# A two-layer trunk on one core: head and tail in another order, three gate tiles, memory values in other PSUM tiles, and the inverse copied in other pieces

## The chip, the core and the metric

The kernel runs on one core of one Trainium2 chip. A core has five engines that run side by side: TensorE (PE, matmul, with PEld for its weight loads), VectorE (DVE), ScalarE (ACT), GpSimd (POOL) and SyncE (SP, which issues the transfers here). The metric is the device time of one execution in microseconds; the kernel before takes 1491.95 us (median of three runs, 1491.53 to 1492.02).

## The reference

The input x is 512 tokens by 1024, the memory is 256 tokens by 1024, all in f32. Two layers follow each other. Cut to what is computed:

```python
for l in range(2):
    h = x @ w_in[l]                      # columns shared out to four branches, their gates and the merge gates
    y_rwkv = _rwkv7_branch(...)          # delta-rule state, 8 heads of 64
    y_mla  = _mla_branch(...)            # latent attention, 8 heads, rotary key
    y_conv = _conformer_conv_branch(...) # GLU, causal convolution of width 31, layer norm, silu
    y_mem  = _memory_xattn_branch(xq, xg, mem, xattn_w_mem_kv[l])   # k, v = mem @ w_mem_kv
    branches = jnp.stack([y_rwkv, y_mla, y_conv, y_mem], axis=2)
    proj   = jnp.einsum('bsnc,ncd->bsnd', branches, w_o_branch[l])
    gates  = jax.nn.sigmoid(merge.reshape(B, S, N_BRANCH, D) + b_gate[l])
    merged = jnp.sum(gates * proj, axis=2)
    x = _layer_norm(DEEPNORM_ALPHA * x + merged @ w_out[l], ln_g[l], ln_b[l])
```

## The kernel before

**Order of the work.** The class Plan (line 67) is a planner. The kernel is written as many small generators (tasks); the planner keeps one clock for each of PE, ACT, DVE and POOL, adds a cost for each operation, and always takes the task that is due next. The order that comes out is the program order on each engine. A plan.spawn(task) hands in a task, plan.t is the time from which it is due, and a yield gives the turn back. So an edit of a cost, a due time or a yield can move instructions far from it. How an engine really waits is decided by semaphores that the framework puts in between.

**Products.** Every f32 matrix is split into a high half (rounded to f32r) and a low half (the rest), and a product is three matmuls, high by low, high by high and low by high. Weights arrive by SP into a raw tile (tag wr, two of them); weights (line 437) then splits them: ACT casts w..h, DVE subtracts w..l. The tiles of x become xh and xl in the same way. The first weight, w0, arrives in two halves in one raw tile, w00 and w01; these and w1 to w7 are the latent projection pl, whose eight steps k use w and x of the same number k (w0's halves stand for k = 0 and 1, and w1 for k = 2 and 3, and so on).

**PSUM.** Three pools share the eight banks: pp (2 banks), pa (2) and pg (4, or 2 while the RWKV branch runs with its small matmuls). A PSUM tile is free for the next user when the engine that reads it is done.

**The memory branch.** Key products (ps_mk) and value products (pmv) of layer 2 are computed at the end of layer 1, by keys and values (line 604). Each product is split from PSUM by ACT (kmh, vmh) and DVE (kml, vml).

**Gates.** In each layer 32 merge gates go through `gate`: a projection ps_m, then a tanh on ACT into a tile tm of tag tg. When the branch's output projection po is done, DVE forms (tm + 1) po, for the first branch into merged, for the others into a tile mt of tag mt, which it adds to merged right after. Tag tg has two tiles and is used by the GLU of the convolution (tglu) and the branch gates too; tag mt has two and is used by the rotary key (kr) as well.

**RWKV in chunks.** In each of eight units the inverse of a small triangular matrix is built by products: x0 gives P and its transpose PT, x1 gives PP and QQ, x2 gives Zi and a half of RA. The other parts (BP, the other half of RA) come from y0. These are read from PSUM by ACT and DVE in turn. State products S come from w on DVE, and tk is PE's transpose of v into the bank that S frees.

**The end of a layer.** `norm` (line 1812) runs per block tb of 128 tokens: pz, the output projection, is added to z by DVE in four quarters, statistics are taken (lbs, lmv), POOL computes lrs, the reciprocal standard deviation, DVE then lnb, and ACT, DVE and POOL apply lrs, ln_g and ln_b. In layer 1 the result is stored and transposed (xT) to be the x of layer 2; in layer 2 each quarter z31, say (block 3, quarter 1), is stored.

## Time and profile before

| | |
|---|---|
| median of three runs | 1491.95 us |
| the profiled execution | 1492.32 us |
| its span, first to last instruction | 1490.5 us |
| granted clock of TensorE, mean | 0.998 |
| busy in the span | PE 1472.6, DVE 1044.7, ACT 678.5, POOL 141.4 us |
| DMA | 153.5 MB, mean 103 GB/s |

In the rows of the profile, a row of the time line begins with the start in us and the duration; several instructions of one form in a row are put together with their count, and in brackets stands the idle time of the engine before it and what ended it. A row of the waits gives the total, the number and the longest. Tiles are named without their numbers: w0l in the time line can be either half of w0.

### The profile page before, as it was taken

To read this page: it belongs to the slowest core of one execution; us is meant where nothing else is said; L and a number is where in the kernel's file an instruction comes from. 1 tells how busy PE (TensorE), PEld (TensorE's weight loads), DVE (VectorE), ACT (ScalarE), POOL (GpSimd) and SP (SyncE) were. 2 spreads that over 40 slices of the span, in tenths; PEclk is the share of its full clock that TensorE was granted. 3 is DMA by queue.
4 is the path that set the end of the run, shared out by engine and by line. 5 is a ranking of instruction groups with operands and counts; after the bars stand their busy time and mean duration, and the time that the engine had idled before them with its cause. 6 is when DMAs were issued, how large, how long until landed. Compare 5 with 4: busy or idle time off the path is not lost.

```text
span 1490.5 us, 28989 instructions
## 1 busy us (share of the span) xinstructions
PE 1472.6 (99%) x11818; PEld 1233.5 (83%) x11818; DVE 1044.7 (70%) x1983; ACT 678.5 (46%) x1299; POOL 141.4 (9%) x329
## 2 busy tenths in 40 slices
PE   9999999999999999999999999999999999999997
PEld 8888888888888887888989888888888788888886
DVE  5799998755756666545554899987766477756747
ACT  5546653425354533443265465623454354444332
POOL 0000000020403030000000000000031103121002
PEclk9999999999999999999999999999999999999999
DMA  6444342332232232434353253332332313234431
GB/s 215 138 124 101 87 122 86 98 81 90 72 84 73 91 82 83 135 118 130 100 164 111 86 133 78 102 106 94 89 95 76 95 50 106 76 95 129 155 102 68
DMA packets 89157, 153.50 MB, mean 103 GB/s; under 512 B 41024, under 2 KB 47424, under 8 KB 89024
## 3 DMA queue, kind: packets, MB, share of 16 engines
q1 hardware_dynamic: 89024, 151.65, 34.5%
q8 instruction: 93, 1.52, 0.4%
q14 instruction: 40, 0.33, 0.1%
HBM read 134.32 MB, written 5.77 MB: 94 GB/s over the span
## 4 chain that ended last, share of the span: by engine, by line
PE 89%; DVE 5%; DMA 2%; ACT 1%; POOL 1%; issue 1%; SPq 0%; ACTq 0%; DVEq 0%; POOLq 0%
PE ps_m L286 24%; PE po L286 12%; PE ps_cg L286 3%; PE ps_xg L286 3%; PE ps_xq L286 3%; PE ps_rg L286 3%; PE ps_mg L286 3%; PE ps_v L286 3%; PE ps_val L286 3%; PE ps_r L286 2%; PE ps_glu L286 2%; PE ps_k L286 2%; PE pz L286 2%; PE ms L286 2%; PE pl L286 2%; PE x L286 1%
## 5 line engine op out<-in xcount | busy, mean ns | idle before, releaser
L235 DVE SCALAR_TENSOR_TENSOR cacc<-hpad,prm,cacc 128x512 f32<-128x512 f32 x240 | 179.0, 748 | 4.0
L235 ACT ACTIVATE tm<-ps_m,prm 128x512 f32<-128x512 f32 x64 | 44.0, 688 | 162.5 <-PE ps_m L286 142.9
L235 DVE SCALAR_TENSOR_TENSOR mt<-tm,po 128x512 f32<-128x512 f32 x48 | 32.9, 686 | 90.2 <-PE po L286 90.2
L235 ACT ACTIVATE mP<-ms,nmm 128x128 f32<-128x128 f32 (+3 forms) x64 | 33.8, 528 | 22.5 <-DVE nmm L235 17.6
L235 POOL TENSOR_TENSOR tmpW<-ZT,W 64x14 f32<-64x14 f32 (+6 forms) x112 | 42.0, 375 | 8.0
L235 POOL TENSOR_TENSOR ZT<-ZT,tmpW 64x14 f32<-64x14 f32 (+6 forms) x112 | 38.6, 344 | 8.8
L235 POOL TENSOR_SCALAR ZT<-W 64x256 f32<-64x256 f32 x8 | 5.6, 698 | 354.4 <-DMA W<-scr 312.5
L235 DVE TENSOR_TENSOR merged<-merged,mt 128x512 f32<-128x512 f32 x48 | 33.3, 694 | 1.7
L235 ACT COPY mPT<-mt 128x128 f32<-128x128 f32 (+3 forms) x64 | 26.8, 426 | 15.1 <-PE mt L291 14.2
L235 POOL MEMSET D<- 128x8 f32 x8 | 0.9, 116 | 332.9 <-PE ms L286 316.9
L235 DVE TENSOR_REDUCE nmm<-ms 128x1 f32<-128x128 f32 (+3 forms) x64 | 30.8, 485 | 0.1
L235 DVE SCALAR_TENSOR_TENSOR merged<-tm,po 128x512 f32<-128x512 f32 x16 | 11.0, 686 | 26.0 <-PE po L286 23.7
L291 PE MATMUL mt<-cst,mP 128*128 128x128 f32 x160 | 27.8, 275 | 0.3 <-ACT mP L235 0.2
L235 POOL TENSOR_SCALAR lrs<-lmv 128x1 f32<-128x1 f32 x8 | 3.6, 447 | 254.1 <-DVE lmv L235 252.7
L235 DVE TENSOR_SCALAR mP<-mP,smm 128x128 f32<-128x128 f32 (+3 forms) x64 | 24.8, 387 | 2.3
L235 POOL TENSOR_SCALAR gr<-gm 128x8 f32<-128x8 f32 x8 | 3.7, 462 | 231.0 <-DVE gm L235 231.0
L235 ACT ACTIVATE z<-z,lnb,lrs 128x256 f32<-128x256 f32 (+1 forms) x16 | 9.6, 647 | 30.3 <-DVE lnb L235 30.3
L235 ACT ACTIVATE yb<-yb,mr,gr 128x64 f32<-128x64 f32 x64 | 22.1, 431 | 2.4 <-DVE mr L235 2.4
L291 PEld LDWEIGHTS mt<-cst,mP 128*128 128x128 f32 x160 | 18.9, 141 | 5.0 <-issue 1.2
L286 PE MATMUL ms<-kTl,qT 96*128 96x128 f32 (+3 forms) x64 | 22.0, 344 | 0.0
L235 ACT ACTIVATE xP<-xs,nmx 128x256 f32<-128x256 f32 x32 | 15.2, 475 | 12.1 <-DVE nmx L235 8.3
L286 PE MATMUL ms<-kTh,qT 96*128 96x128 f32 (+3 forms) x64 | 20.6, 322 | 0.0
(3541 smaller groups left out, 5257.8 us busy)
## 6 DMA issues: line engine op xcount, KB each, us to landing
w<-in_w_ch_dram SPq DMA_DIRECT2D x146, 512.0 KB, 3.7
w<-in_w_o_dram SPq DMA_DIRECT2D x32, 512.0 KB, 3.6
w<-in_w_out_dram SPq DMA_DIRECT2D x16, 512.0 KB, 3.5
w<-in_w_lat_dram SPq DMA_DIRECT2D x15, 336.0 KB, 3.2
w<-in_w_mk_dram SPq DMA_DIRECT2D x8, 512.0 KB, 3.5
w<-in_w_mv_dram SPq DMA_DIRECT2D x8, 512.0 KB, 4.0
w<-in_w_qk_dram SPq DMA_DIRECT2D x8, 320.0 KB, 3.0
x<-in_xT_dram SPq DMA_DIRECT2D x8, 256.0 KB, 6.4
```

The source lines that it names most:

```text
L235: return self.plan.keep(f(*a, **k))
L286: plan.keep(nc.tensor.matmul(o, lhsT, rhs, start=start, stop=stop))
L291: plan.keep(nc.tensor.transpose(o, i, ident))
```

## The change

It has eight edits.

- **Head:** the halves of w0 are split when each has landed, as two tasks of their own, and w1 is split in two halves too; before, the second half of w0 came after x1, and w1 was split whole.
- **Memory values of layer 2** take two tiles of pg instead of two of pp. The latent item nb = 0 of layer 2 takes pp and pa, and waits until eight transposed x tiles have been read (`turned`); nb = 1 takes pg.
- **Normalization of layer 1:** plan.t is moved 700 ns on before lnb.
- **Inverse:** P, PT, Zi and the half of RA are copied by the index c2 instead of s: ACT takes c2 = 0 and DVE c2 = 1 of each. c2 is the PSUM bank of x0 and x2.
- **BP and RA:** both BP products come before both copies of RA, instead of one after the other.
- **Convolution:** yc is read from PSUM first and ctn is computed from yc, so PSUM is read once, not twice.
- **Tiles:** tag tg has three tiles, tag mt one, and kr takes the small tiles u.
- **Tail:** in layer 2 a block's quarters 0 and 1 (0, 1 and 2 in the last block) are centred and scaled by ln_g on DVE before lrs is awaited, and finished by a second operation; quarter 3 goes to ACT and POOL, in the last block a half of it, the other half to DVE. Quarter 2 of the other blocks goes to ACT and DVE.

```diff
...
             e = 0
-            if last or first:
+            if last:
                 for i, (w, c) in enumerate(zip(ws, parts)):
-                    if first:
-                        plan.t = max(plan.t, plan.done[f"w0{i}"][0])
-                        yield
...
-        plan.spawn(run(), plan.done["w00" if first else raw.tensor.name][0])
+        left = [2]
+
+        def half(i, c):
+            h, lo = (u(f"{name}{n}{i}", c, F32R) for n in "hl")
+            yield from split(h, lo, raw[:, c * i:c * i + c])
+            ws[i].extend((h, lo))
+            left[0] -= 1
+            if left[0] == 0:
+                wlive["raw"] -= 1
+
+        if name in ("w0", "w1"):
+            for i, c in enumerate(parts):
+                plan.spawn(half(i, c), plan.done[f"w0{i}" if first else raw.tensor.name][0])
+        else:
+            plan.spawn(run(), plan.done[raw.tensor.name][0])
...
     X = [[] for _ in range(LAYERS + 1)]
+    turned = [0]
...
         def values(get):
-            ps = [pp.tile([128, 512], F32, tag="pp", name=f"pmv{i}_{l}") for i in range(1 + (l > 0))]
-            if l == 0:
+            if l:
+                ps = yield from pg.take([128, 512], f"pmv{l}", 2)
+            else:
+                ps = [pp.tile([128, 512], F32, tag="pp", name=f"pmv0_{l}")]
...
                     yield from keep("v", i, slice(0, 512), ps[i])
+                    if l:
+                        pg.free()
...
             P, PT = rk("T", [2, 4, 64], "P"), rk("PT", [2, 4, 64])
-            for s in SUB:
-                S.copy(chunks(P[:, s]), x0[:, 0, s])
-                V.tensor_copy(chunks(PT[:, s]), x0[:, 1, s])
+            for x, q in ((P, 0), (PT, 1)):
+                for c2, copy in ((0, S.copy), (1, V.tensor_copy)):
+                    copy(x.rearrange("p s (a b) w -> p b s a w", b=2)[:, c2], x0[:, q, :, c2])
...
                 yield
+                for s in SUB:
+                    V.tensor_tensor(out=by2(BP[s])[:, :, :, 64:128], in0=y0[:, 0, s],
+                                    in1=cc("minc").unsqueeze(1).unsqueeze(1).to_broadcast([128, 2, 2, 64]), op=ALU.mult)
...
                     S.copy(by2(RA[s])[:, :, :, 64:128], y0[:, 1, s].rearrange("p h c w -> p c h w"))
-                    V.tensor_tensor(out=by2(BP[s])[:, :, :, 64:128], in0=y0[:, 0, s],
-                                    in1=cc("minc").unsqueeze(1).unsqueeze(1).to_broadcast([128, 2, 2, 64]), op=ALU.mult)
...
             Z = rk("Z", [2, 4, 64], "Zi")
-            for s in SUB:
-                S.copy(chunks(Z[:, s]), x2[:, 0, s])
-                V.tensor_copy(by2(RA[s])[:, :, :, 0:64], x2[:, 1, s])
+            for c2, copy in ((0, S.copy), (1, V.tensor_copy)):
+                copy(Z.rearrange("p s (a b) w -> p b s a w", b=2)[:, c2], x2[:, 0, :, c2])
+                for s in SUB:
+                    copy(by2(RA[s])[:, c2, :, 0:64], x2[:, 1, s, c2])
...
                 t, z = u(f"ctn{i}" + t_), u(f"yc{i}" + t_)
-                S.activation(t, ps, AF.Tanh, scale=hp("cln_g", i), bias=hp("cln_b", i))
...
                 pa.free()
+                S.activation(t, z, AF.Tanh, scale=0.5)
...
             def glu(ps):
-                d["t"] = sp.tile([128, 512], F32, tag="tg", name=f"tglu{i}" + t_)
+                d["t"] = sp.tile([128, 512], F32, tag="tg", bufs=3, name=f"tglu{i}" + t_)
...
             def run(get):
-                if nb == 0:
+                if nb == l:
...
                 else:
+                    if nb == 0:
+                        yield lambda: turned[0] == 8
...
                         S.copy(latq[tb][:, 0:336], ps[tb])
-                        pg.free()
...
                         S.copy(L["kpe"][:, 32 * tb:32 * tb + 32], ps[tb][:, 304:336])
-                        if tb > 1:
-                            pa.free()
+                    if nb == l:
+                        pg.free()
+                    elif tb > 1:
+                        pa.free()
...
             yield
-            kr = [sp.tile([32, 512], F32R, tag="mt", name=f"kr{n}" + t_) for n in "hl"]
+            kr = [u(f"kr{n}" + t_, 512, F32R, 32) for n in "hl"]
...
                 def after(ps, i=i):
-                    t = sp.tile([128, 512], F32, tag="tg", name=f"t{name}{i}" + t_)
+                    t = sp.tile([128, 512], F32, tag="tg", bufs=3, name=f"t{name}{i}" + t_)
...
                     ps = yield from project(get, X[l], f"m{n}{d}" + t_)
-                    t = sp.tile([128, 512], F32, tag="tg", name=f"tm{n}{d}" + t_)
+                    t = sp.tile([128, 512], F32, tag="tg", bufs=3, name=f"tm{n}{d}" + t_)
...
                         else:
-                            mt = sp.tile([128, 512], F32, tag="mt", name=f"mt{n}{d}" + t_)
+                            mt = sp.tile([128, 512], F32, tag="mt", bufs=1, name=f"mt{n}{d}" + t_)
...
                 rstd_of(rs, mv[:, 1:2], 1.0, 16.0 * LN_EPS)
+                if not last:
+                    plan.t += 700.0
+                near = 2 + (tb == 3)
+                if last:
+                    gs, bs = ([cut(E["ab"][2 * n:2 * n + 2], i) for i in range(zn)] for n in range(2))
+                    for i in range(near):
+                        V.scalar_tensor_tensor(out=z[tb][i], in0=z[tb][i], scalar=mv[:, 0:1], in1=gs[i], op0=ALU.subtract, op1=ALU.mult)
+                    plan.due(rs)
...
                 if last:
-                    for i in (3, 1, 2):
-                        S.activation(z[tb][i], z[tb][i], AF.Identity, scale=rs, bias=nb)
-                    y, g, b = z[tb][0], cut(E["ab"][:2], 0), cut(E["ab"][2:], 0)
-                    V.scalar_tensor_tensor(out=y, in0=y, scalar=mv[:, 0:1], in1=g, op0=ALU.subtract, op1=ALU.mult)
-                    V.scalar_tensor_tensor(out=y, in0=y, scalar=rs, in1=b, op0=ALU.mult, op1=ALU.add)
-                    plan.spawn(store(tb, 0))
-                    for i, eng in ((3, G), (1, V), (2, V)):
-                        y, g, b = z[tb][i], cut(E["ab"][:2], i), cut(E["ab"][2:], i)
-                        eng.tensor_tensor(out=y, in0=y, in1=g, op=ALU.mult)
-                        eng.tensor_tensor(out=y, in0=y, in1=b, op=ALU.add)
-                        plan.spawn(store(tb, i))
+                    ways = [(i, slice(0, zw), "V" if i < near else "G" if i == 3 else "AV") for i in (3, 0, 1, 2)]
+                    if tb == 3:
+                        ways = [(3, slice(128, 256), "G"), *ways[1:], (3, slice(0, 128), "V2")]
+                    for i, c, way in sorted(ways, key=lambda x: x[0] * (-1 if tb < 2 else 1)):
+                        if way in ("G", "AV"):
+                            S.activation(z[tb][i][:, c], z[tb][i][:, c], AF.Identity, scale=rs, bias=nb)
+                    for i, c, way in ways:
+                        y, g, b = z[tb][i][:, c], gs[i][:, c], bs[i][:, c]
+                        if way == "V2":
+                            V.scalar_tensor_tensor(out=y, in0=y, scalar=mv[:, 0:1], in1=g, op0=ALU.subtract, op1=ALU.mult)
+                        if way[0] == "V":
+                            V.scalar_tensor_tensor(out=y, in0=y, scalar=rs, in1=b, op0=ALU.mult, op1=ALU.add)
+                        else:
+                            eng = G if way == "G" else V
+                            eng.tensor_tensor(out=y, in0=y, in1=g, op=ALU.mult)
+                            eng.tensor_tensor(out=y, in0=y, in1=b, op=ALU.add)
+                        if tb < 3 or way != "G":
+                            plan.spawn(store(tb, i))
...
                 pa.free()
+                turned[0] += 1
...
```

DVE's program at the head. xl0 and xl1 are the low halves of x tiles 0 and 1, w0l0 and w0l1 the low halves of w0's two parts. Before:

```order
L235 TENSOR_TENSOR xl0_0_141<-x00_123,xh0_0_140 128x512
L235 TENSOR_TENSOR w0l0_148<-w0_132,w0h0_147 128x336
L235 TENSOR_TENSOR xl1_0_157<-x01_124,xh1_0_156 128x512
L235 TENSOR_TENSOR w0l1_160<-w0_132,w0h1_159 128x336
L235 TENSOR_TENSOR xl2_0_177<-x02_125,xh2_0_176 128x512
L235 TENSOR_TENSOR w1l_181<-w1_137,w1h_180 128x672
```

After:

```order
L235 TENSOR_TENSOR xl0_0_141<-x00_123,xh0_0_140 128x512
L235 TENSOR_TENSOR w0l0_148<-w0_132,w0h0_147 128x336
L235 TENSOR_TENSOR w0l1_156<-w0_132,w0h1_155 128x336
L235 TENSOR_TENSOR xl1_0_161<-x01_124,xh1_0_160 128x512
L235 TENSOR_TENSOR xl2_0_179<-x02_125,xh2_0_178 128x512
L235 TENSOR_TENSOR w1l0_183<-w1_137,w1h0_182 128x336
L235 TENSOR_TENSOR w1l1_186<-w1_137,w1h1_185 128x336
```

w0l1 now stands ahead of xl1, and w1l is in two parts.

DVE's program in the unit of layer 2 at whose end PE's tk stands, with the engine that each row waits for. PT, BP, QQ and PP belong to the inverse, S1 and S2 are the state (S2's bank is the one tk waits for), mt13 and merged3 belong to a merge gate. Before:

```order
L235 COPY PT_1_0_1_12872<-x0_1_0_1_12798 128x2x2x64 [waits Activation_49] x2
L235 SCALAR_TENSOR_TENSOR S1_1_0_0_12879<-w1_1_0_0_12865,dl_1_0_0_11454,H_1_0_0_12280 128x64 [waits PE_49]
L235 SCALAR_TENSOR_TENSOR S1_1_0_0_12879<-w1_1_0_0_12865,dl_1_0_0_11454,H_1_0_0_12280 128x64
L235 SCALAR_TENSOR_TENSOR mt13_1_12888<-tm13_1_12753,po13_1_12791 128x512 [waits PE_49]
L235 TENSOR_TENSOR merged3_1_11098<-merged3_1_11098,mt13_1_12888 128x512 [waits DVE_49]
L235 TENSOR_TENSOR BP0_1_0_1_12574<-x0_1_0_1x_12799,cst_81 128x4x64 [waits Activation_49]
L235 TENSOR_TENSOR BP1_1_0_1_12575<-x0_1_0_1x_12799,cst_81 128x4x64 [waits Activation_49]
L235 TENSOR_TENSOR QQ_1_0_1_12935<-x1_1_0_1_12891,Q_1_0_1_12756 128x512 [waits PE_49]
L235 TENSOR_TENSOR PP_1_0_1_12934<-x1_1_0_1_12891,cst_81 128x512
L235 SCALAR_TENSOR_TENSOR S2_1_0_0_12938<-w2_1_0_0_12897,dl_1_0_0_11454,H_1_0_0_12280 128x64 [waits PE_49]
```

After:

```order
L235 COPY P_1_0_1_12885<-x0_1_0_1_12812 128x4x64 [waits Activation_49]
L235 COPY PT_1_0_1_12886<-x0_1_0_1_12812 128x4x64 [waits Activation_49]
L235 SCALAR_TENSOR_TENSOR S1_1_0_0_12893<-w1_1_0_0_12879,dl_1_0_0_11466,H_1_0_0_12294 128x64 [waits PE_49]
L235 SCALAR_TENSOR_TENSOR S1_1_0_0_12893<-w1_1_0_0_12879,dl_1_0_0_11466,H_1_0_0_12294 128x64
L235 SCALAR_TENSOR_TENSOR mt13_1_12902<-tm13_1_12767,po13_1_12805 128x512 [waits DVE_49,PE_49]
L235 TENSOR_TENSOR merged3_1_11110<-merged3_1_11110,mt13_1_12902 128x512 [waits DVE_49]
L235 TENSOR_TENSOR BP0_1_0_1_12588<-x0_1_0_1x_12813,cst_81 128x4x64
L235 TENSOR_TENSOR BP1_1_0_1_12589<-x0_1_0_1x_12813,cst_81 128x4x64
L235 TENSOR_TENSOR QQ_1_0_1_12949<-x1_1_0_1_12905,Q_1_0_1_12770 128x512 [waits PE_49]
L235 TENSOR_TENSOR PP_1_0_1_12948<-x1_1_0_1_12905,cst_81 128x512
L235 SCALAR_TENSOR_TENSOR S2_1_0_0_12952<-w2_1_0_0_12911,dl_1_0_0_11466,H_1_0_0_12294 128x64 [waits PE_49]
```

The rows BP0 and BP1 no longer wait for ACT (Activation), mt13 now waits for DVE too, and the copies of P and PT still wait for ACT. In the same unit's ACT program both RA copies stand behind both BP, where the first stood ahead of them.

DVE's program at the end of layer 2, from the last block's add of z33 on. Before:

```order
L235 TENSOR_TENSOR z33_1_15389<-z33_1_15389,pz13256_1_16235 128x256
L235 BN_STATS lbs3_1_16078<-z33_1_15389 128x6
L235 BN_AGGR lmv3_1_16264<-lbs3_1_16078 128x2
L235 TENSOR_TENSOR z22_1_15384<-z22_1_15384,ln_g1_1_1_15584 128x256
L235 TENSOR_TENSOR z22_1_15384<-z22_1_15384,ln_b1_1_1_15629 128x256
L235 SCALAR_TENSOR_TENSOR lnb3_1_16275<-lmv3_1_16264,lrs3_1_16265 128x1
L235 SCALAR_TENSOR_TENSOR z30_1_15386<-z30_1_15386,lmv3_1_16264,ln_g0_1_1_15560 128x256
L235 SCALAR_TENSOR_TENSOR z30_1_15386<-z30_1_15386,lrs3_1_16265,ln_b0_1_1_15601 128x256
L235 TENSOR_TENSOR z31_1_15387<-z31_1_15387,ln_g0_1_1_15560 128x256
L235 TENSOR_TENSOR z31_1_15387<-z31_1_15387,ln_b0_1_1_15601 128x256
L235 TENSOR_TENSOR z32_1_15388<-z32_1_15388,ln_g1_1_1_15584 128x256
L235 TENSOR_TENSOR z32_1_15388<-z32_1_15388,ln_b1_1_1_15629 128x256
```

After:

```order
L235 TENSOR_TENSOR z33_1_15409<-z33_1_15409,pz13256_1_16246 128x256
L235 BN_STATS lbs3_1_16098<-z33_1_15409 128x6
L235 BN_AGGR lmv3_1_16285<-lbs3_1_16098 128x2
L235 SCALAR_TENSOR_TENSOR z30_1_15406<-z30_1_15406,lmv3_1_16285,ln_g0_1_1_15580 128x256
L235 SCALAR_TENSOR_TENSOR z31_1_15407<-z31_1_15407,lmv3_1_16285,ln_g0_1_1_15580 128x256
L235 SCALAR_TENSOR_TENSOR z32_1_15408<-z32_1_15408,lmv3_1_16285,ln_g1_1_1_15604 128x256
L235 SCALAR_TENSOR_TENSOR lnb3_1_16295<-lmv3_1_16285,lrs3_1_16286 128x1
L235 SCALAR_TENSOR_TENSOR z30_1_15406<-z30_1_15406,lrs3_1_16286,ln_b0_1_1_15621 128x256
L235 SCALAR_TENSOR_TENSOR z31_1_15407<-z31_1_15407,lrs3_1_16286,ln_b0_1_1_15621 128x256
L235 SCALAR_TENSOR_TENSOR z32_1_15408<-z32_1_15408,lrs3_1_16286,ln_b1_1_1_15649 128x256
L235 SCALAR_TENSOR_TENSOR z33_1_15409<-z33_1_15409,lmv3_1_16285,ln_g1_1_1_15604 128x128
L235 SCALAR_TENSOR_TENSOR z33_1_15409<-z33_1_15409,lrs3_1_16286,ln_b1_1_1_15649 128x128
```

Three STT that need only the mean (lmv3) moved ahead of lnb3, the first row that needs lrs3; behind lnb3 stand three STT of 256 columns and two of 128 instead of two STT and four TT.

More of the change, by code (lines that the diff above doesn't have):

```diff
@@ L969, in others @@
                 for s in SUB:
-                    S.copy(by2(RA[s])[:, :, :, 64:128], y0[:, 1, s].rearrange("p h c w -> p c h w"))
                     V.tensor_tensor(out=by2(BP[s])[:, :, :, 64:128], in0=y0[:, 0, s],
                                     in1=cc("minc").unsqueeze(1).unsqueeze(1).to_broadcast([128, 2, 2, 64]), op=ALU.mult)
+                for s in SUB:
+                    S.copy(by2(RA[s])[:, :, :, 64:128], y0[:, 1, s].rearrange("p h c w -> p c h w"))
                 pg.free()
```

## The prediction

> **What bounds the kernel now.** I read the page's busy times first, then the waits of PE, then the time line around each wait and around the end of the span.
>
> ```profile
> span 1490.5 us, 28989 instructions
> PE 1472.6 (99%) x11818; PEld 1233.5 (83%) x11818; DVE 1044.7 (70%) x1983; ACT 678.5 (46%) x1299; POOL 141.4 (9%) x329
> ...
> PE tk L291 <- DVE S L235: 1.8, 1, 1.8
> PE pmv L286 <- DVE kml L235: 1.2, 1, 1.2
> PE pl L286 <- DVE w0l L235: 0.9, 1, 0.9
> PE po L286 <- DVE merged L235: 0.8, 1, 0.8
> PE w L286 <- DVE S L235: 0.4, 1, 0.4
> PE pl L286 <- DVE w2l L235: 0.2, 1, 0.2
> ```
>
> PE is busy for 1472.6 of 1490.5 us, so 17.9 us is all that any reordering can win while PE's 9340 program rows stay as they are, and they do: the change neither removes nor adds a matmul. Each row of the waits is one event. What is left of the 17.9 lies mostly after PE's last matmul (10.2 us, in the part on the tail). So the prediction is a sum of a few named holes, and the question at each is what is late next. The sum is made against the profiled execution (span 1490.5, 1492.32 us in all, so 1.8 us lie around the span); the median, 1491.95, is 0.37 lower, and I take that off at the end. A difference of 0.2% is 2.98 us: that is about what a measurement of this kernel tells from no change.
>
> **Head.** Both halves of w0 are now split before x1, and w1 is split in two halves.
>
> ```profile
> 12.47 0.62 ACT L235 CAST xh<-x 128x512 fp32r<-128x512 f32 x1
> 13.33 0.75 ACT L235 CAST w2h<-w 128x672 fp32r<-128x672 f32 x1 [0.24 <-DMA w<-in_w_lat_dram]
> 7.73 0.69 DVE L235 TENSOR_TENSOR xl<-x,xh 128x512 fp32r<-128x512 f32 x1 [2.10 <-ACT xh L235]
> 8.34 0.50 DVE L235 TENSOR_TENSOR w0l<-w,w0h 128x336 fp32r<-128x336 f32 x1
> 11.93 1.89 DVE L235 TENSOR_TENSOR xl<-x,xh 128x512 fp32r<-128x512 f32 x3
> 14.12 0.86 DVE L235 TENSOR_TENSOR w2l<-w,w2h 128x672 fp32r<-128x672 f32 x1 [0.30 <-ACT w2h L235]
> 15.03 0.42 PE L286 MATMUL pl<-w2l,xh 128*128 128x336 f32 x1 [0.21 <-DVE w2l L235]
> ```
>
> DVE waits 2.10 us for x1 with the second half of w0 behind it; after, that half runs inside the wait, and PE's 0.89 us before it goes. But PE then reaches w2l early and waits there: w2l ends at 14.98, and PE starts at 15.03. So only an earlier w2l counts. Its transfer is issued when w0's raw tile is free, now some 2.4 us earlier, but behind all x tiles in SP's queue as before; w2h cannot start before the last xh ends (13.09 instead of 13.33), and w2l not before the last xl (13.82 instead of 14.12). The gain is therefore between 0 (the transfer lands as late as now) and 0.30. I take 0.25, since SP's queue has nothing else between. If the whole 0.89 and 0.21 went, it would be 1.1; the xl row at 11.93 excludes that unless the x tiles land earlier too.
>
> **Layer boundary.** The values of layer 2 (pmv) take two banks of pg, so they don't wait for the bank that the key products hold until kml is written; the last blocks' normalization (lnb, z) is planned 700 ns later; the latents pl take the freed banks.
>
> ```profile
> 753.61 0.81 ACT L235 ACTIVATE z<-z,lnb,lrs 128x512 f32<-128x512 f32 x1 [2.33 <-DVE lnb L235]
> 754.33 0.35 ACT L235 CAST kmh<-ps_mk 128x256 fp32r<-128x256 f32 x1
> 755.19 1.05 ACT L235 CAST w124h<-w 128x1024 fp32r<-128x1024 f32 x1 [0.52 <-DMA w<-in_w_mv_dram]
> 756.63 0.78 ACT L235 ACTIVATE xf<-xT,prm 128x512 f32<-128x512 f32 x1 [0.39 <-PE xT L291]
> 754.71 0.42 DVE L235 TENSOR_TENSOR kml<-ps_mk,kmh 128x256 fp32r<-128x256 f32 x1 [0.68 <-ACT kmh L235]
> 768.63 0.86 DVE L235 TENSOR_TENSOR w127l<-w,w127h 128x672 fp32r<-128x672 f32 x1
> 769.54 0.42 PE L286 MATMUL pl<-w127l,xh 128*128 128x336 f32 x1
> ```
>
> The wait of 1.2 us ended with kml. It goes, but from 756.63 on ACT runs xf, xh and weight casts nearly without a gap until w127h, and PE's pl starts 0.05 us after w127l ends. So PE's gain is only what ACT's run starts earlier. PE sent ACT its first xT 0.39 us after w124h's cast had ended; with PE 1.2 us earlier this wait goes and leaves w124h, which waits 0.52 us for its own transfer. So the gain is 0.39, to which comes what the transfer brings: between 0 and 0.52, since stores of z that now stand beside it move behind it. At the low end there is 0, if the later z30 holds the transposes back; at the high end 1.2, the whole wait. I take 0.6, nearest to 0.39 with half of the transfer's 0.52.
>
> **Three gate tiles, one mt.**
>
> ```profile
> 986.96 0.69 ACT L235 ACTIVATE tm<-ps_m,prm 128x512 f32<-128x512 f32 x1 [7.32 <-DVE merged L235]
> 986.18 0.69 DVE L235 SCALAR_TENSOR_TENSOR merged<-tm,po 128x512 f32<-128x512 f32 x1 [0.68 <-PE po L286]
> ...
> L235 DVE SCALAR_TENSOR_TENSOR mt<-tm,po 128x512 f32<-128x512 f32 x48 | 32.9, 686 | 90.2 <-PE po L286 90.2
> ```
>
> One gate tile is held by tglu3 and the other by tm30, so the tanh of gate 31 stands behind merged, 7.32 us idle, and its PSUM bank with it; PE's 0.8 us before po ends at the same place. With a third tile that tanh runs when its projection is done, the bank is free, and the hole goes: gain 0.8 (0.9 with the slow start of the matmul behind it, 0.50 instead of 0.39), nothing late next. The third tile is paid with one mt tile. On DVE the writer of mt waits 90.2 us in 48 pieces for PE, 1.9 us each, and its reader follows at once on the same engine, so the second mt buffer covers nothing: cost 0. The kr tiles that shared its tag take two of the small tiles, once per layer: 0.
>
> **Inverse in other pieces.** P and PT are copied by c2 (a PSUM bank each for ACT and DVE), Zi and RA likewise; both BP products now come ahead of both RA copies.
>
> ```profile
> 1183.90 0.37 ACT L235 COPY RA<-x_1x 128x256 f32<-128x256 f32 x1 [2.25 <-DVE BP L235]
> 1183.45 0.42 DVE L235 TENSOR_TENSOR BP<-x_1x,cst 128x256 f32<-128x256 f32 x1
> 1184.30 0.42 DVE L235 TENSOR_TENSOR BP<-x_1x,cst 128x256 f32<-128x256 f32 x1 [0.44 <-ACT RA L235]
> 1185.84 0.47 DVE L235 SCALAR_TENSOR_TENSOR S<-w,dl,H 128x64 f32<-128x64 f32 x2
> ```
>
> The largest wait, tk at 1186.45 (1.8 us), ends with this S. DVE stood 0.44 us between the two BP for ACT's RA; in the built program the BP now wait for nothing of ACT's, so QQ, PP and S come 0.44 to 0.5 earlier, and tk with them. I take 0.5. The low end is 0 (the products of QQ come late), the high end 1.8, if all that precedes S shrinks. ACT's RA copies fall behind BP and the cast w194h about 0.6 later, with its reader w194l behind S anyway: 0. The copies of P and PT still wait, each for the other engine's copy before it (the built program has these waits), so four copies stay a chain: 0, between −0.3 and +0.3 for the other shape of a piece. The 0.4 before w (again behind S) stays. In Z/RA DVE's copies wait for ACT's last: 0 too. The convolution's transposes, read once: the second activation reads SBUF instead of PSUM, off PE's path, 0.
>
> The Trainium skill, "PSUM — Partial Sum Buffer", section "Specifications (TRN2)", says that ScalarE and VectorE read PSUM in parallel at full bandwidth as long as they don't meet in a bank. By it the pieces cut by bank could run side by side, and the sum would be some 0.8 better (two handovers of about 0.4). The sum does without it, because of the waits.
>
> **Tail.**
>
> ```profile
> 1480.05 0.28 PE L286 MATMUL pz<-w237h,mg7l 128*128 128x256 f32 x1
> 1480.68 0.83 DVE L235 TENSOR_TENSOR z<-z,ln_b 128x256 f32<-128x256 f32 x1
> 1481.43 0.41 DVE L235 TENSOR_TENSOR z<-z,pz 128x256 f32<-128x256 f32 x1
> 1482.51 0.36 DVE L235 TENSOR_TENSOR z<-z,ln_g 128x256 f32<-128x256 f32 x1
> 1483.00 0.74 POOL L235 TENSOR_TENSOR lrs<-lrs,mhalf 128x1 f32<-128x1 f32 x1
> 1483.85 0.48 DVE L235 SCALAR_TENSOR_TENSOR z<-z,lmv,ln_g 128x256 f32<-128x256 f32 x1
> 1485.10 0.62 DVE L235 TENSOR_TENSOR z<-z,ln_g 128x256 f32<-128x256 f32 x1 [0.24 <-ACT z L235]
> 1486.95 0.42 DVE L235 TENSOR_TENSOR z<-z,ln_b 128x256 f32<-128x256 f32 x1
> ```
>
> PE ends at 1480.33. The last add waits behind the block before it until 1481.43, POOL's lrs ends at 1483.74, DVE ends at 1487.37, and 3.1 us of store follow. After lrs DVE has two STT and four TT, 3.6 us. Now two STT (three in the last block) with the mean come while POOL computes lrs, so after lrs remain lnb, three STT of 256 and two of 128. At 0.42 a whole and 0.37 a half (from 0.48 each, which overlap when they don't depend) this is 0.1 + 1.26 + 0.75 = 2.1, a gain of 1.5. In block 2 the same turn takes two STT out of the time after its lrs, about 0.6 before the last add: 2.1 together. POOL works beside the last STT, and a TT beside POOL took 0.62 and 0.83 instead of 0.36 and 0.42. That is 0.67 of slowing in POOL's 1.6 us; for the half tile that POOL now has, 0.3. So 1.8. The low end is 1.2 (nothing won in block 2, slowing doubled), the high end 2.7 (no slowing, and the last add at once at 1480.4).
>
> The Trainium skill, "SBUF — State Buffer", section "Who interferes with whom", goes further: a DVE instruction with two SBUF inputs and a GpSimd instruction that reads SBUF exclude each other for the whole instruction. By that, DVE would stand for all of POOL's time on its half, an estimated 0.8, and the tail would win 1.3. The rows above show less than that (0.67 in 1.6 us), so it stays a case inside the range.
>
> **Sum.** 0.25 + 0.6 + 0.85 + 0.5 + 1.8 = 4.0 us: 1492.32 − 4.0 = 1488.3 for an execution like the profiled one, and 0.37 less, 1487.95, for the median. I say **1487.9**.
>
> **Rivals.**
> - More goes: the w124 transfer lands early (boundary 1.2), S gains most of its 1.8 (say 1.2), the tail reaches 2.4, with 0.3 and 0.85: 5.95, that is 1486.0. For it speaks that all these holes are in the waits; against it, that each has a second wait close behind. Chance 0.15.
> - The inner holes only move, since later work of ACT and DVE is full (as at w2l): only the tail's 1.8 stays, 1490.15, or 1490.75 with the tail's low end. This counts as the same. Chance 0.22.
> - Slower: mt's single tile. If its 48 writers have to wait for the add before them in earnest, by 0.2 us each and all of it on PE's path, that is 9.6: 1491.95 − 4.0 + 9.6 = 1497.55. It decides from 4.0 / 48 = 0.08 us a piece on, and is slower by 0.2% from (4.0 + 2.98) / 48 = 0.15. The built program has the new wait, DVE on itself. Against it stand the 1.9 us for which DVE waits for PE at each piece. Chance 0.08, the share for a new wait in the reordered gate projections with it.
> - The forecast, from 1486.5 (between it and the first rival) to 1489.1 (between it and the second): 0.55.
>
> **How the numbers follow.** Faster by over 0.2% means under 1488.97: nearly all of the forecast (0.53), and the first rival: 0.68. The same: the second rival and the rest of the forecast, 0.24. Slower: 0.08. The range reaches over the forecast and the first two rivals, with 0.8 below the first for its own spread, and leaves out the third: from 1485.2 to 1490.8.
>
> **What would show it.** In the changed kernel's waits of PE: pmv behind kml and po behind merged are gone; pl behind w2l grows to about 0.85 (0.89 + 0.21 − 0.25) and pl behind w0l is gone; tk behind S shrinks to about 1.3. DVE shows no 0.44 between BP's two rows and still one between P's and PT's. After PE's last matmul stand 8.4 us instead of 10.2. I am wrong if a wait of over 1 us stands in PE's list that is not there now (a ps_m, a po or an xT), or if DVE's rows in the last 3 us before the stores are as long as 0.62 and 0.83 each.

## The result, and the profile after

The changed kernel takes 1488.24 us (median of 14 runs, 1487.16 to 1489.58), the kernel before 1492.03 (14 runs): a ratio of 0.9973, 95% interval 0.9966 to 0.998. It is 3.8 us faster; 4.0 were forecast. The profiled execution took 1488.66 us with a span of 1486.5, against 1492.32 and 1490.5. The four microseconds of the spans divide into 2.44 up to the end of PE's last matmul (1480.33 before, 1477.89 after) and 1.56 behind it. The time around the span grew by 0.3: 1.8 us before, 2.1 in the runs of the changed kernel. The forecast took it as unchanged.

The page's first lines and PE's waits, of the kernel after:

```profile
span 1486.5 us, 29014 instructions
PE 1472.0 (99%) x11818; PEld 1232.9 (83%) x11818; DVE 1043.4 (70%) x1994; ACT 675.6 (45%) x1303; POOL 144.2 (10%) x329
...
PE tk L291 <- DVE S L235: 1.2, 1, 1.2
PE pl L286 <- DVE w2l L235: 0.8, 1, 0.8
PE w L286 <- DVE S L235: 0.8, 1, 0.8
PE pl L286 <- ACT xh L235: 0.5, 1, 0.5
PE ps_val L286 <- DVE w11l L235: 0.5, 1, 0.5
```

PE's work is the same; the waits behind kml and merged are gone, that behind the largest S is shorter, and w2l's and the other S's are longer. Place by place, the gain against the kernel before in the two profiles. PE's position is read at the same matmul in both, and 0.13 us that PE won between 422 and 750 us stand in no row of the table.

| place | forecast | gained there, by the trace |
|---|---|---|
| head, until 15 us | 0.25 | 0.25 |
| head, after 50 us | 0.25 | 0.0 |
| layer boundary, 755 to 770 us | 0.6 | 0.66 |
| gate tiles, 985 us | 0.85 | 1.08 |
| tk, 1184 us | 0.5 | 0.55 |
| PE's last matmul | 2.2 | 2.44 |
| tail | 1.8 | 1.56 |
| outside the span | 0 | −0.3 |

**Head.** The wait for w2l in the kernel after, and PE's first matmul with w11l, in the kernel before and (second fence) after:

```profile
50.49 0.50 PE L286 MATMUL ps_val<-xh,w11l 128*128 128x512 f32 x1 [0.51 <-DVE w11l L235]
```

```profile
14.78 0.42 PE L286 MATMUL pl<-w2l,xh 128*128 128x336 f32 x1 [0.82 <-DVE w2l L235]
...
50.54 0.50 PE L286 MATMUL ps_val<-xh,w11l 128*128 128x512 f32 x1 [0.53 <-DVE w11l L235]
48.18 1.05 ACT L235 CAST w11h<-w 128x1024 fp32r<-128x1024 f32 x1 [1.81 <-DMA w<-in_w_ch_dram]
```

PE was 0.25 us ahead after w2l. At w11l it stands at the same time in both kernels, because ACT's cast waits 1.81 us for the transfer of w11. That transfer was issued 0.25 us earlier than before (43.44 instead of 43.69), but took 4.72 us to land instead of 4.42. In the fourteen traces of this document it takes between 4.27 and 4.86, so one pair of traces doesn't show whether the 0.25 would always be lost here. At 422 us the wait of w behind S stands in both profiles: the matmul began at 421.68 before and at 421.70 after, with the idle time in front of it grown from 0.42 to 0.78.

**Layer boundary.** ACT of the kernel after:

```profile
753.19 0.37 ACT L235 CAST kmh<-ps_mk 128x256 fp32r<-128x256 f32 x1 [0.82 <-PE ps_mk L286]
753.73 0.82 ACT L235 ACTIVATE z<-z,lnb,lrs 128x512 f32<-128x512 f32 x1 [0.16 <-DVE lnb L235]
754.54 1.05 ACT L235 CAST w124h<-w 128x1024 fp32r<-128x1024 f32 x1
755.49 0.77 ACT L235 ACTIVATE xf<-xT,prm 128x512 f32<-128x512 f32 x1
```

The run of xf and xh begins at 755.49 instead of 756.63, with no wait for w124 or for PE. PE wins 1.21 us by 756 and keeps 0.66 of it at 770. Between 760 and 769 us it gives back 0.55; ACT waits there 0.24 for the transfer of w126.

**Gate tiles.** PE at the hole before, and (second fence) gate 31's tanh on ACT, PE at the same place and the page's row of mt, after:

```profile
985.75 0.39 PE L286 MATMUL po<-yxg3h,w160l 128*128 128x512 f32 x1
986.92 0.50 PE L286 MATMUL po<-yxg0l,w160h 128*128 128x512 f32 x1 [0.78 <-DVE merged L235]
```

```profile
982.56 0.69 ACT L235 ACTIVATE tm<-ps_m,prm 128x512 f32<-128x512 f32 x1 [3.81 <-PE ps_m L286]
...
984.86 0.39 PE L286 MATMUL po<-yxg3h,w160l 128*128 128x512 f32 x1
985.08 0.39 PE L286 MATMUL po<-yxg0l,w160h 128*128 128x512 f32 x1
...
L235 DVE SCALAR_TENSOR_TENSOR mt<-tm,po 128x512 f32<-128x512 f32 x48 | 32.9, 686 | 89.8 <-PE po L286 89.7
```

The tanh waits for its projection alone, and po follows without a gap. The gain is more than the idle 0.78, because PE's rows overlap: without a wait the second row begins 0.22 us behind the first, before it began 1.17 behind it. That is 0.95, and nearly all of the rest stands in the two starts behind it. The writer of mt waits 89.8 us for PE as it did before (90.2), so one mt tile costs nothing that shows.

**tk.** PE before, then DVE and PE of the kernel after:

```profile
1186.45 0.63 PE L291 MATMUL tk<-cst,v 128*128 128x128 f32 x4 [1.76 <-DVE S L235]
```

```profile
1181.47 0.75 DVE L235 TENSOR_TENSOR BP<-x_1x,cst 128x256 f32<-128x256 f32 x2
1183.33 0.47 DVE L235 SCALAR_TENSOR_TENSOR S<-w,dl,H 128x64 f32<-128x64 f32 x2
...
1183.94 0.63 PE L291 MATMUL tk<-cst,v 128*128 128x128 f32 x4 [1.21 <-DVE S L235]
```

The two BP products run in a row, S comes 1.86 us after the first of them instead of 2.39, and tk waits 1.21 instead of 1.76.

**Tail.** The last block's statistics on DVE and three rows of POOL, before; then (second fence) PE's last matmul, DVE and POOL, after:

```profile
1482.33 0.26 DVE L235 BATCH_NORM_AGGREGATE lmv<-lbs 128x2 f32<-128x24 f32 x1
...
1480.44 0.79 POOL L235 TENSOR_TENSOR z<-z,ln_b 128x256 f32<-128x256 f32 x1
1482.68 0.23 POOL L235 TENSOR_SCALAR lrs<-lmv 128x1 f32<-128x1 f32 x1 [1.46 <-DVE lmv L235]
...
1484.65 0.79 POOL L235 TENSOR_TENSOR z<-z,ln_g 128x256 f32<-128x256 f32 x1 [0.91 <-ACT z L235]
```

```profile
1477.61 0.28 PE L286 MATMUL pz<-w237h,mg7l 128*128 128x256 f32 x1
...
1478.54 0.41 DVE L235 TENSOR_TENSOR z<-z,pz 128x256 f32<-128x256 f32 x1
1479.45 0.27 DVE L235 BATCH_NORM_AGGREGATE lmv<-lbs 128x2 f32<-128x24 f32 x1
1479.75 1.33 DVE L235 SCALAR_TENSOR_TENSOR z<-z,lmv,ln_g 128x256 f32<-128x256 f32 x3
1481.20 1.47 DVE L235 SCALAR_TENSOR_TENSOR z<-z,lrs,ln_b 128x256 f32<-128x256 f32 x3
1482.59 0.54 DVE L235 SCALAR_TENSOR_TENSOR z<-z,lmv,ln_g 128x128 f32<-128x128 f32 x1
1483.17 0.35 DVE L235 SCALAR_TENSOR_TENSOR z<-z,lrs,ln_b 128x128 f32<-128x128 f32 x1
...
1479.29 0.72 POOL L235 TENSOR_TENSOR z<-z,ln_b 128x256 f32<-128x256 f32 x1
1480.09 0.25 POOL L235 TENSOR_SCALAR lrs<-lmv 128x1 f32<-128x1 f32 x1
1480.42 0.67 POOL L235 TENSOR_TENSOR lrs<-lrs,mhalf 128x1 f32<-128x1 f32 x1
1481.89 0.50 POOL L235 TENSOR_TENSOR z<-z,ln_g 128x128 f32<-128x128 f32 x1 [0.80 <-ACT z L235]
1482.47 0.52 POOL L235 TENSOR_TENSOR z<-z,ln_b 128x128 f32<-128x128 f32 x1
```

From lrs to DVE's end it is now 2.43 us (1481.09 to 1483.52) instead of 3.63: 1.2 won. The last add stands 0.65 us behind PE's end instead of 1.10: 0.45 won. But lrs starts 0.37 us after the statistics (1479.72) and not 0.09, with POOL at block 2's quarter until 1480.01, and ends 1.37 behind them instead of 1.15: 0.22 lost. The run with POOL's quarter first, below, shows that POOL's being late is not most of this. The store takes 0.15 less.

### The profile page after: what moved, and what is told of

Its sections match the earlier page's. It is cut to its first block, busy times and chain, and to the rows that moved or that the text cites. A ratio compares the mean times of both kernels' runs of the same rounds, so it can differ in the third digit from the quotient of the medians.

```text
span 1486.5 us, 29014 instructions
## 1 busy us (share of the span) xinstructions
PE 1472.0 (99%) x11818; PEld 1232.9 (83%) x11818; DVE 1043.4 (70%) x1994; ACT 675.6 (45%) x1303; POOL 144.2 (10%) x329
## 4 chain that ended last, share of the span: by engine, by line
PE 91%; DVE 4%; ACT 1%; DMA 1%; POOL 1%; issue 1%; SPq 0%; DVEq 0%; ACTq 0%; POOLq 0%
PE ps_m L286 24%; PE po L286 12%; PE ps_cg L286 3%; PE ps_xg L286 3%; PE ps_rg L286 3%; PE ps_xq L286 3%; PE ps_mg L286 3%; PE ps_glu L286 3%; PE ps_v L286 3%; PE ps_val L286 3%; PE ps_r L286 2%; PE pz L286 2%; PE ps_k L286 2%; PE ms L286 2%; PE pl L286 2%; PE x L286 1%
## 5 line engine op out<-in xcount | busy, mean ns | idle before, releaser
L235 DVE SCALAR_TENSOR_TENSOR mt<-tm,po 128x512 f32<-128x512 f32 x48 | 32.9, 686 | 89.8 <-PE po L286 89.7
L235 ACT ACTIVATE z<-z,lnb,lrs 128x256 f32<-128x256 f32 (+2 forms) x11 | 7.0, 666 | 30.3 <-DVE lnb L235 30.3
```

What stands on the lines that cost most here:

```text
L235: return self.plan.keep(f(*a, **k))
```

## The experiments

Each of the three groups of runs has the kernel before on its own chip beside it (1491.21, 1491.27, 1491.34 us; the last run 1491.14). Each kernel takes 0.7 to 0.9 us less on these chips than on the chip of the result (1492.03 and 1488.24 there), and the 95% interval of a ratio reaches some 0.1%, 1.5 us, to either side. So medians are given as differences to before on the same chip, and a difference of less than about 1 us between two variants is read from the position of PE in their traces. Time around the span is 2.1 to 2.2 us in four of these runs (the changed kernel again, without the BP edit, with the double read, with POOL's quarter first) and 1.8 in the eight others; no run tells which edit costs this. The changed kernel, run again, gives this yardstick.

> The changed kernel unaltered, on the chip of the three runs that follow, to compare their traces with. 3.2 to 4.4 us under the kernel before on the same chip.

Measured: 1487.32, that is 3.95 under before (ratio 0.9972, 0.996 to 0.9983), PE's end at 1476.32 and 8.6 us behind it. The wait of w at 422 us, 0.78 in the profile after, isn't there.

**Tail undone**: `norm` of the last layer as before, the rest as changed.

> The changed kernel with the tail of before: a block of the last layer is normalized as it was, everything else as changed. Theory (the tail is worth what the traces show, 10.2 us after PE's last matmul before against 8.6 after): 1.6 us slower than the changed kernel, about 1489.8, with 10.0 to 10.3 us after PE's last matmul. Prediction's own term: 1.8, 1490.0. Rival (the tail's gain is mostly fewer PE waits elsewhere): under 0.5 us slower, 1488.5.

Measured: 1489.18, 2.03 under before, so 1.8 to 1.9 slower than the changed kernel; behind PE's last matmul (1477.04, span 1487.3) stand 10.2 us. The tail is worth 1.6 in the trace, and the rival is out.

**Boundary undone**: pmv in pp, and no 700 ns.

```diff
-            if l:
-                ps = yield from pg.take([128, 512], f"pmv{l}", 2)
+            ps = [pp.tile([128, 512], F32, tag="pp", name=f"pmv{i}_{l}") for i in range(1 + (l > 0))]
...
-                if not last:
-                    plan.t += 700.0
```

> The changed kernel with the memory values of layer 2 in pp again and without the 700 ns. Theory (0.73 us: the 1.2 us wait goes, ACT's run behind it gives back the rest): 0.7 slower than the changed kernel, about 1488.95, and a wait pmv behind kml of 1.2 us in PE's list. Rival 1 (the whole wait was won): 1.2 slower, 1489.45. Rival 2 (only moved): within 0.2.

Measured: 1488.15, 3.06 under before, so 0.7 to 0.9 slower than the changed kernel. PE's list has pmv behind kml again:

```profile
PE pmv L286 <- DVE kml L235: 1.2, 1, 1.2
```

Against the changed kernel run again, at the same matmuls, PE is 1.19 us behind at 757 us, 1.04 at 770 and 1.14 at 800. So the boundary is worth about 1.0 to 1.1 there, nearer to the first rival's 1.2 than to the theory's 0.7. In time it is less than that because this run has 0.3 less around its span. The 0.66 of the profile after is the smallest case: the nine other traces with the whole edit keep 0.86 to 1.10 against the kernel before.

**The 700 ns alone undone**, with pmv in pg.

```diff
-                if not last:
-                    plan.t += 700.0
```

> The changed kernel without the 700 ns in the normalization of layer 1; pmv stays in pg. Theory (pmv's other tiles are what took the 1.2 us wait away; the 700 ns only puts kmh ahead of z30 on ACT, where nobody waits for kmh any more): level with the changed kernel within 0.3. Rival (the later z stores free the transfer of w124, the 0.52 us that ACT waited for it): 0.3 to 0.5 slower, with ACT's cast w124h later.

Measured: 1488.77, 2.50 under before: 1.3 to 1.45 slower than the changed kernel, and slower than with the whole boundary edit undone. The theory is out, and the rival's size too. ACT of the changed kernel run again, and (second fence) without the 700 ns:

```profile
753.58 1.03 ACT L235 CAST w124h<-w 128x1024 fp32r<-128x1024 f32 x1
754.51 0.77 ACT L235 ACTIVATE xf<-xT,prm 128x512 f32<-128x512 f32 x1
```

```profile
752.61 0.81 ACT L235 ACTIVATE z<-z,lnb,lrs 128x512 f32<-128x512 f32 x1 [2.33 <-DVE lnb L235]
754.17 0.78 ACT L235 ACTIVATE xf<-xT,prm 128x512 f32<-128x512 f32 x1 [0.48 <-PE xT L291]
755.50 1.05 ACT L235 CAST w124h<-w 128x1024 fp32r<-128x1024 f32 x1
...
PE xT L291 <- ACT xf L235: 0.9, 1, 0.9
PE pmv L286 <- DVE w126l L235: 0.8, 1, 0.8
```

Two things come together. Two stores of z are issued 0.6 and 1.0 us after w124's transfer instead of 2.0 and 2.4, and it lands 4.5 us after its issue (754.23) instead of 3.8 (753.29). And the planner puts the first xf ahead of w124h, which starts 1.9 us later; PE then waits for xf and for w126l, and is 0.7 us behind at 760 us and 1.9 from 765 on. Which of the two weighs more was not tried. So the pg tiles without the 700 ns cost 0.6 (2.50 against 3.06 under before); the 700 ns without the pg tiles was not run.

**Gates alone** on the kernel before: three tg, one mt, kr in the small tiles.

```diff
-                    t = sp.tile([128, 512], F32, tag="tg", name=f"tm{n}{d}" + t_)
+                    t = sp.tile([128, 512], F32, tag="tg", bufs=3, name=f"tm{n}{d}" + t_)
...
-                            mt = sp.tile([128, 512], F32, tag="mt", name=f"mt{n}{d}" + t_)
+                            mt = sp.tile([128, 512], F32, tag="mt", bufs=1, name=f"mt{n}{d}" + t_)
```

> The kernel before with nothing but three gate tiles, one mt tile and kr in the small tiles. Theory: the hole before po goes, PE's last matmul comes 0.85 to 1.1 us earlier, 1491.0 to 1491.2; nothing else moves, for the single mt costs nothing. Rival (the single mt tile holds DVE, and PE behind it): slower than before, by 9.6 at 0.2 us a piece, 1501.6.

Measured: 1490.34, 0.87 under before. PE gains 1.08 in one step at 985 us, the same as in the changed kernel. The single mt tile costs nothing that can be seen, and the slower rival is out by 11 us. The ratio alone, 0.9994 with an interval of 0.9984 to 1.0004, would not show a gain; the step in the trace does.

**Head undone.**

> The changed kernel with w0 and w1 split as before. Theory (the head's gain is swallowed by the waits for w11l at 50 us and for S at 422 us, which stand at the same times in both traces): PE is 0.0 to 0.3 us later at 15 us, and level with the changed kernel from 50 or 422 us on; the time is within 0.3 of 1488.24. Rival (the prediction's term): 0.25 us slower from the head to the end. The time alone can't tell these apart, the positions in the trace can.

Measured: 1486.89, 4.32 under before: not slower than the changed kernel, and level with it within the span, for 0.3 of the difference lie around the span. PE waits 1.3 us for w0l, but its matmul with w2l begins at 14.79, where the kernel after has 14.78. In the three traces without the head's edit this matmul begins at 15.03, 14.63 and 14.79, in the eleven with it between 14.66 and 15.16. So already at 15 us a gain of 0.25 can't be told from the scatter. Its wait for w11l:

```profile
50.48 0.50 PE L286 MATMUL ps_val<-xh,w11l 128*128 128x512 f32 x1 [0.53 <-DVE w11l L235]
```

The same time as in the two kernels above. In all fourteen traces this matmul starts between 50.12 and 50.84, in the three without the head's edit between 50.48 and 50.66: no gain of the head is left here that these traces could show.

**BP and RA alternating again**, and **the convolution's second read of PSUM back**:

> The changed kernel with BP and RA alternating as before. Theory (DVE's 0.44 us between the two BP products was all that this edit took from the wait of tk): the wait tk behind S is 1.6 to 1.8 us instead of 1.2, and the time 0.4 to 0.5 above the changed kernel's. Rival (other edits shortened that wait): 1.2 stays, and the time is the same.

> The changed kernel with the convolution's transposes read from PSUM twice, ctn first, as before. Theory (after the run without the BP edit, where tk was released by yc at the same 1.2 us: each of the two edits alone is enough for tk): tk still waits 1.2 us, for S; the time is within 0.3 of the changed kernel's. Rival (the single read is what shortened the wait): tk waits 1.7 and the time is 0.5 higher.

Measured: 1487.81 (3.46 under before) and 1487.33 (4.01 under). Both still wait 1.2 us at tk. Without the BP edit, in the first of them:

```profile
1182.99 0.66 PE L291 MATMUL tk<-cst,v 128*128 128x128 f32 x4 [1.24 <-ACT yc L235]
...
1182.88 0.47 DVE L235 SCALAR_TENSOR_TENSOR S<-w,dl,H 128x64 f32<-128x64 f32 x2
```

tk starts before S has ended: here its PSUM bank comes from yc, which reads cb for the last time once the transposes are read only once. With the double read and the BP edit it waits for S, as in the changed kernel. So each edit alone takes the 0.55 from the wait, and the second adds nothing. In the first run the rival's 1.2 came true and the time is still 0.49 above the changed kernel's, as the theory had it. But by PE's position only 0.05 of that stands at tk; the rest stands at 50, 1195 and 1340 us, where other traces wander too, and its cause is open. The theory of the second run held.

**Pieces undone**: P, PT, Zi and RA copied by s.

> The changed kernel with P, PT, Zi and the half of RA copied by s as before. Theory (the copies wait for each other in both cuts): no wait of PE differs by over 0.2 us, and the time is within 0.3 of the changed kernel's. Rival (the cut by bank lets ACT and DVE read at the same time, two handovers of 0.4 less): 0.4 to 0.8 slower, with a longer wait of x or w at 422 and 566 us.

Measured: 1487.54, 3.73 under before; no wait of PE at 422 or 566 us. That is 0.22 above the changed kernel (0.6 within the span). One unit differs: at 1264 us a product of PE starts 0.28 us later, which the two other traces copied by s don't show. The copies of ACT and DVE overlap in time in neither cut. So the other cut is worth nothing that these runs can tell from their scatter.

**POOL's quarter first in block 2.**

```diff
-                    for i, c, way in sorted(ways, key=lambda x: x[0] * (-1 if tb < 2 else 1)):
+                    for i, c, way in sorted(ways, key=lambda x: x[0] * (-1 if tb < 3 else 1)):
```

> The changed kernel with only the tail's edit of the former: ACT does block 2's quarter 3 ahead of quarter 2. Theory (POOL is still at that quarter when the last statistics are ready, which cost lrs 0.3 us): lrs starts within 0.1 of the statistics, and 8.3 us stand after PE's last matmul instead of 8.6. Rival (DVE then waits for quarter 2, and the last add comes later by as much): 8.6 to 9.0.

Measured: 1488.45, 2.89 under before, 9.6 us behind PE's last matmul. The rival's mechanism holds, beyond its 8.6 to 9.0. lrs does start early, 0.09 us behind the statistics, but DVE now has this ahead of the last add:

```profile
1477.23 0.56 DVE L235 TENSOR_TENSOR z<-z,ln_g 128x256 f32<-128x256 f32 x1 [0.37 <-ACT z L235]
1477.83 0.83 DVE L235 TENSOR_TENSOR z<-z,ln_b 128x256 f32<-128x256 f32 x1
1478.58 0.41 DVE L235 TENSOR_TENSOR z<-z,pz 128x256 f32<-128x256 f32 x1
...
1479.84 0.48 POOL L235 TENSOR_SCALAR lrs<-lmv 128x1 f32<-128x1 f32 x1 [1.46 <-DVE lmv L235]
```

It waits 0.37 us for ACT, and its two operations run beside POOL's, 0.56 and 0.83 instead of 0.42 and 0.43 in the changed kernel. The last add stands 1.65 us behind PE's end instead of 0.65. And the early lrs wins little: its first operation takes 0.48 us instead of 0.25 and ends, as in the kernel after, 0.05 behind the first of DVE's three STT with the mean, so that lrs ends 1.32 us behind the statistics instead of 1.37. Of the 0.22 that lrs lost against before, POOL's other work explains 0.05; the rest is the price of the STT that the edit moved ahead of lnb.

**Four edits more, then three.** ACT copies its pieces of P and PT in a row, then DVE its own; RA is copied before BP; S2 goes ahead of QQ in the unit where tk waits; and the edit of POOL above, which the second run leaves out. The second also holds w3 back.

```diff
-            for x, q in ((P, 0), (PT, 1)):
-                for c2, copy in ((0, S.copy), (1, V.tensor_copy)):
+            for c2, copy in ((0, S.copy), (1, V.tensor_copy)):
+                for x, q in ((P, 0), (PT, 1)):
...
+                    S.copy(by2(RA[s])[:, :, :, 64:128], y0[:, 1, s].rearrange("p h c w -> p c h w"))
+                for s in SUB:
...
+            if t == "_1_0_1":
+                plan.t += 600.0
...
+                    if t == "_1_0_0" and c == 2:
+                        plan.t += 1200.0
```

> The changed kernel and four edits more: ACT copies its pieces of P and PT in a row and DVE its own after that (one handover instead of three); both RA copies before both BP products; S2 ahead of QQ and PP in the one unit where tk waits for it; in block 2 of the last layer ACT serves POOL's quarter first, so that POOL is free for the last block's lrs. Theory: the 1.2 us before tk go, the waits of x and w at 566 and 422 us are shorter by up to 0.4 and 0.14, and lrs starts 0.3 us earlier in the tail: 1.5 to 2.1 under the changed kernel. Rival (the wait of tk moves to the x behind it, which needs vt from ACT): 0.5 to 0.8 under it.

> The changed kernel with three of the four edits (POOL's quarter is again as changed), and the state product w3 held back until x2, so that PE's 64 by 64 matmuls are again one stretch there. Theory (of the 1.2 us won before tk the run with four edits lost 0.6 to the further switch between 128 by 128 and 64 by 64 matmuls, and 0.9 in the tail to the edit of POOL): PE's last matmul comes 1.0 to 1.5 us earlier than in the changed kernel run again (1476.3), with 8.6 to 8.7 us after it; the time is 1.0 to 1.5 under the changed kernel's. Rival (the 1.2 us are given back by the next wait whatever stands there): 0.6 or less.

Measured with four: 1487.70, 3.64 under before. PE no longer waits at tk, but its last matmul is only 0.45 us earlier than in the changed kernel run again, and 9.9 us follow it. PE there:

```profile
1182.39 0.45 PE L286 MATMUL w<-S,Gs 64*64 64x64 f32 x8 [0.24 <-ACT yc L235]
1182.77 0.50 PE L286 MATMUL ps_m<-xl,w192h 128*128 128x512 f32 x1
```

w3 is now a stretch of 64 by 64 matmuls of its own, with a wait of 0.24 in front, where it had followed x2 in one stretch. With w3 held back and POOL's edit left out, 1485.66 (five runs), 5.48 under before: ratio 0.9961, 0.9947 to 0.9975. tk follows cb at once,

```profile
1180.70 0.60 PE L291 MATMUL cb<-cst,cn 128*128 128x128 f32 x4
1181.29 0.63 PE L291 MATMUL tk<-cst,v 128*128 128x128 f32 x4
```

and PE's last matmul ends at 1475.00, 1.32 us before that of the changed kernel run again, so the theory holds for PE. Behind it 8.9 us follow and not 8.6 to 8.7, for the last store takes 3.3 us instead of 3.0. This version is the fastest of those run, 1.5 to 1.7 us ahead of the changed kernel when each is held against before on its chip; 0.3 of that lie around the span.

## Why the prediction was right

The forecast of 1487.9 was 0.3 us off, and four of the five terms of the sum stand at the places and with the waits that it named. That the total came so close is partly luck: the head's 0.25, 0.24 of the tail and 0.3 outside the span were missing, and the gates, the boundary, tk and 0.13 elsewhere brought 0.5 more than was said. The waits that it named as signs are as said: pmv behind kml, po behind merged and pl behind w0l are gone, tk waits 1.2 us (1.3 said), no new wait is over 1 us, and 8.6 us follow PE's last matmul (8.4 said). By its steps:

- **Head, 0.25.** The wait moved to w2l, 0.82 us long where 0.85 was said. That w2l then came 0.25 earlier is so in the profile after, but within the scatter of the fourteen traces. "Only an earlier w2l counts" named the next late tile and stopped there; at w11l, which waits for its own transfer, nothing of the gain is left. The term came out at 0.
- **Layer boundary, 0.6.** 0.66 in the profile after, by the mechanism named: the wait goes and ACT's run behind it gives back the rest. But the term was sized too low: the nine other traces keep 0.86 to 1.10, near the 0.39 and the whole 0.52 of the transfer together, where half of the transfer was taken. The run without the 700 ns shows that this term also had a low end below the 0 that the prediction gave it: the edit without its 700 ns costs 0.6 net (2.50 under before against 3.06).
- **Gate tiles, 0.85.** 1.08. The term was read from the idle time and the longer row, 0.9 at most; the time from one start to the next, 1.17 instead of 0.22, gives 0.95 at this place and the rest at the two matmuls behind it. One mt tile costs nothing, as said.
- **S and tk, 0.5.** 0.55, but the reason was only half the story. The step "read once ... off PE's path, 0" was wrong as a separate statement: without the BP edit the single read shortens the wait as much, since yc then frees the bank that tk takes.
- **Pieces, 0.** Right by the waits: in the profile after none of ACT's 40 copies runs at the same time as one of DVE's 40. Undoing them changed nothing that the runs can tell from scatter. The Trainium skill's rule on parallel reads of PSUM ("PSUM — Partial Sum Buffer", section "Specifications (TRN2)") had no chance to act, since DVE's copies still waited for ACT's in every unit.
- **Tail, 1.8.** 1.56. The part behind lrs was right (1.2, with 0.33 of slowing beside POOL where 0.3 was said: three STT take 1.47 instead of 1.33, a half one 0.54 instead of 0.35). Mis-sized was what block 2 gives, 0.45 instead of 0.6, and left out was that lrs ends 0.22 later behind the statistics. The reading of the slowing was wrong, and its size came out by luck. It is no share of POOL's time: a DVE row with two inputs in SBUF that comes while a row of POOL runs ends a fixed time behind the end of POOL's row. For 256 columns that is 0.28 us: 1485.72 behind 1485.44 and 1481.51 behind 1481.23 before, 1482.67 behind 1482.39 after; for 128 columns 0.14 (1483.13 behind 1482.99). DVE's add of z and pz, with one input in PSUM, took 0.41 us beside POOL as without it (1478.54 after). The Trainium skill, "SBUF — State Buffer", section "Who interferes with whom", says that a DVE instruction with two SBUF inputs contends with a GpSimd instruction that reads SBUF. These rows agree with it, as an exclusion of whole rows: what DVE loses depends on how much of POOL's row is left when it comes, and it was 0.33 us here, not all of POOL's 1.02.

The second rival (inner holes only move) is out by the run with the tail undone: it is still 2.03 us under before (ratio 0.9987, 0.9978 to 0.9997). The slower one is out by the run with the gates alone.

## What to carry to other kernels

For each hole that an edit closes, go on to the next wait of that engine that ends with a transfer: the head's gain was no longer to be seen at w11l, 35 us behind it. A hole whose bank can come from one of two readers (here S or yc, as the planned order has it) is shortened by either edit, and terms for both must not be added. Read what a hole costs from the starts of the rows around it and not from the idle time alone, since rows overlap (0.95 instead of 0.78 at the gate tiles). For DVE rows beside POOL rows, go by the rest of POOL's row and not by a share of its time. In a program that a planner orders, an edit of one due time moves stores and casts with it, so look for what is issued beside the next weight's transfer. And set the time outside the span beside the span: here it took back 0.3 of some 4 us.

## What the runs showed that was not expected

- A weight tile of 512 KB, w124, landed 3.75 to 4.03 us after its issue in the ten traces with the next stores 1.7 to 2.05 us behind it, and 4.44 to 4.68 in the four with them 0.5 to 0.8 us behind it.
- Eight 64 by 64 matmuls in a stretch of their own cost about 0.3 us more than the same eight behind others of their shape (0.62 for the stretch without its wait, against 0.34). With the wait of 0.24 in front these rows took back 0.5 of the 1.2 us won at tk; by PE's position 0.65 were lost.
- The wait of w at 422 us, 0.42 and 0.78 us, stands only in the two profiles from the result's chip and in none of the twelve other traces. In these two the transfer of w70 takes 4.8 to 4.9 us to land, in the others 3.8 to 4.3 (it landed at 417.9 after, at 416.6 in the run again). Such a hole belongs to the run or the chip as much as to the kernel; whether it is the reason why that chip is slower was not tried.
- The changed kernel loses 0.3 us outside its span, 2.1 instead of 1.8 us, and so do three of its variants, while eight others and the kernel before don't. The cause is open.
